# Chunked attention: which products stand between the heads' steps on TensorE, and behind which transposes

## The chip, the core and the metric

The kernel runs on one core of a Trainium2 chip. Five engines work beside each other, each through its own instructions in the order in which they stand: TensorE (PE in the profile) multiplies matrices into PSUM, VectorE (DVE) and ScalarE (ACT) read PSUM and SBUF, GpSimd (POOL) works on SBUF alone, and SyncE (SP) issues the transfers from HBM. An instruction starts when the ones ahead of it on its engine have started and the semaphores that it waits for have been raised. The metric is the device time of one execution in microseconds (us).

## The reference

The program is a network of eight stages on 512 rows of 1024 values. The change lies in the seventh, an attention of 16 heads whose keys and values are shared. In cut form:

```python
def shared_kv(x, kv_norm, w_kv, k_norm):
    h = rmsnorm_2(x, kv_norm)
    kv = (h @ w_kv).reshape(bsz, s, 2, N_HEADS, HEAD_DIM)
    k = rmsnorm_2(kv[:, :, 0], k_norm)
    v = kv[:, :, 1]
...
    def one_chunk(args):
        c, qb = args
        kb = lax.dynamic_slice_in_dim(k_pad, c * CHUNK, BAND, axis=2)
        vb = lax.dynamic_slice_in_dim(v_pad, c * CHUNK, BAND, axis=2)
        sc = jnp.einsum('bhqd,bhkd->bhqk', qb, kb).astype(jnp.float32) * scale + bias
        valid = (c * CHUNK - PAD + jnp.arange(BAND)) >= 0
        sc = jnp.where(valid, sc, -jnp.inf)
        p = jax.nn.softmax(sc, axis=-1).astype(vb.dtype)
        return jnp.einsum('bhqk,bhkd->bhqd', p, vb)
...
            q = (rmsnorm_2(h, b_norm[j]) @ b_w_q[j]).reshape(bsz, s, N_HEADS, HEAD_DIM)
            q = rmsnorm_2(q, b_q_norm[j])
            o = chunk_band_attention(q, k_pad, v_pad, b_rel_bias[j])
            h = h + o @ b_w_o[j]
```

Keys and queries are normed per head, over 64 values: what this norm waits for is at the centre of the prediction.

## The kernel before

Every operand of a product is held as a high and a low part, and `mm3` (lines 148 to 152) makes three matmuls of each product. So a row of line 150, 151 or 152 is a third of a product.

In `attention` (line 883) the 16 heads go in four groups of four; `qt` counts the groups. `quarter` (line 951) makes what a group needs, in steps: `headed(0)` makes the keys, `headed(2)` the queries, `values` the values. Each of the three starts with `project` (line 909), eight steps of twelve matmuls of 256 columns (tiles `ps_mm`, or `ps_s` once) with their weights loaded from HBM, scaled by GpSimd (line 137) and split into high and low parts (lines 140 and 143). After its projection `headed` copies the result out of PSUM (ScalarE, line 917, four copies), squares it (line 920), sums the squares (VectorE, line 921), makes the factors (VectorE line 183, GpSimd line 184), and yields. In its next step it multiplies by the factors (VectorE, line 928, twice) and lets TensorE transpose the two halves into two PSUM tiles (line 933, eight transposes), which are then split into the keys or queries that the heads read. In the same step the next projection begins with its first twelve matmuls.

`heads` (line 326) goes through the 16 steps of a group, four per head with 128, 256, 384 and 512 keys. A step is `scores` (line 269): three matmuls into `ps_s`, the bias and the maximum on VectorE (line 289), the exponentials on ScalarE (line 291), and the division (lines 292 to 296); and, two steps later, `turn` (line 299): transposes of `p` (line 308) into a PSUM tile `ps_t`, its split, and after the fourth step of a head eight matmuls with the values into `ps_o` (line 319). Between them `fill` takes one step of a filler, 36 times per group. The fillers of groups 0 to 2 are `quarter` of the next group; that of group 3 is `values` of group 3 and 48 steps of the output product (`out`, line 964, three matmuls of 512 columns per step).

The tiles `ps_t` have two PSUM buffers that go round in the order of the program; the transposes of line 933 and those of line 308 share them. The tiles `p` have four buffers. What the program's order leaves open is settled by a scheduler when the kernel is built: it takes instructions of higher priority first (the heads' steps have it) and otherwise what it believes to be ready. `issue_after` binds the TensorE instructions made inside it to stand behind a given one. In the kernel before it is used in group 3 alone, from the twentieth step of the filler on. The first and third stages use `heads` too (`mix`, line 361), without it.

Of the kernel before, what the change touches and what calls it, by code (L numbers as in the profile page):

```python
# [65 lines left out]
class Net:  # L66
# [256 lines left out]
            nc.scalar.activation(out=f[a], in_=o[b], func=AF.Copy)  # L323
            it["done"](o[a], f[a], a)

    def heads(self, items, filler, held=99, hi=1000, depth=2):


        pend, marks = [], []

        def turn():
            with self.tc.high_priority(offset=hi):
                self.turn(*pend.pop(0))
            marks.append(self.mark.ins)

        steps = iter(range(99))

        def fill():
            with self.tc.issue_after(marks[-1]) if next(steps) >= held and marks else ExitStack():
                next(filler, None)  # L340

        items[0]["prep"](items[0])
        for n, it in enumerate(items):
            for qb in range(4):
                with self.tc.high_priority(offset=hi):
                    pend.append((it, qb, self.scores(it, qb)))
                fill()
                if len(pend) > depth:
                    turn()
                if qb == 1 and n + 1 < len(items):  # L350
                    items[n + 1]["prep"](items[n + 1])
                fill()
        while pend:
            fill()
            turn()
            fill()
        for _ in filler:
            pass


    def mix(self, l, gnext):
# [10 lines left out]
        with tc.tile_pool(name=f"att{l}", bufs=1, reuse_waits="tile") as ap:  # L372
# [104 lines left out]
            val = [None] * 4  # L477
# [98 lines left out]
            items = [item(hd) for hd in range(8)]  # L576
            prep(items[0])
            items[0]["prep"] = lambda it: None
            gating()
            self.heads(items, branches(), 99, 1000, 2)  # L580
            keep_hp.close()
        with tc.tile_pool(name=f"gate{l}", bufs=1, reuse_waits="tile") as gp:
            self.wide = 0
# [299 lines left out]
    def attention(self, gnext):  # L883
# [3 lines left out]
        with tc.tile_pool(name="att", bufs=1, reuse_waits="tile") as ap:  # L887
# [53 lines left out]
            def values(qt, res):  # L941
                pss = yield from project(1, qt, "mm")
                val = self.t(ap, "v", 2, (P, 4, 2, 4, 64), F32R)
                for i in range(4):
                    if i % 2 == 0:
                        f = self.t(ap, "qr", 3, (P, 2, 4, 64)).rearrange("p n h c -> p n (h c)")
                    S_.activation(out=f[:, i % 2], in_=pss[i // 2][:, i % 2], func=AF.Copy, scale=r[:, i:i + 1])
                    self.split_values(val[:, i], f[:, i % 2])
                res.append(val)

            def quarter(qt, res):
                k, q, v = [], [], []
                yield from headed(0, qt, k)
                yield from headed(2, qt, q)
                res.extend((k, q, v))
                if qt < 3:
                    yield from values(qt, v)

            os_ = [None] * 8
            bias = [self.t(ap, f"bias{n}", 1) for n in range(2)]  # L960
# [3 lines left out]
            def out(k0, nk, c0, n=None):  # L964

                per = 8 // nk
                for i in range(KT):
# [5 lines left out]
                    if n is not None:  # L973
                        self.norm_step(n, i, ALL)

            cur = []
            for _ in quarter(0, cur):
                pass
            for qt in range(4):
                nxt = []  # L980
                k, q, val = cur
                items = []
                for hh in range(4):
                    hd = qt * 4 + hh

                    def prep(it, hd=hd):
                        b = bias[hd % 2]
                        nc.sync.dma_start(out=b[:, 256:], in_=d["bias"][hd])
                        G.tensor_scalar(out=b[:, 256:], in0=b[:, 256:], scalar1=b[:, 256:257], scalar2=None,
                                        op0=ALU.subtract)  # L990
                        G.memset(b[0:64, 448:], NEG)
                        it["bias"] = b

                    def done(o, f, rows, hd=hd):
                        j = hd // 2
                        if hd % 2 == 0:
                            os_[j] = self.pair(ap, "o", 6) if j < 6 else self.pair(ap, "k", 4)
                        V.tensor_tensor(out=f, in0=o, in1=f, op=ALU.add)
                        self.split((os_[j][0][rows], os_[j][1][rows]), f, eng=G)

                    items.append(dict(p=4, step=1 - hh % 2 * 2, q=q[hh // 2], k=k[hh // 2], rows=slice((hh % 2) * 64, (hh % 2) * 64 + 64),
                                      pool=ap, prep=prep, done=done,
                                      v=lambda kb, hh=hh, val=val: val[0][:, kb, hh // 2, hh % 2 * 2:hh % 2 * 2 + 2]))

                def filler():
                    if qt < 3:
                        yield from quarter(qt + 1, nxt)
                    else:
                        yield from values(3, val)
                        yield from out(0, 4, 0)  # L1010
                        yield from out(4, 2, 4)

                self.heads(items, filler(), 20 if qt == 3 else 99, 1000, 2)
                cur = nxt
            n = self.norm_begin(gnext[0])
            for _ in out(6, 2, 6, n):
# [164 lines left out]
```

## Time and profile before

| | |
|---|---|
| time, median of 3 runs | 2823.43 us (2822.30 to 2823.83) |
| the profiled execution | 2822.87 us, of which 2821.1 us are the span of its instructions |
| granted TensorE clock, mean | 0.986 of full speed |
| TensorE busy | 2753.3 us, 98% |
| VectorE, ScalarE, GpSimd busy | 1565.7, 1137.2, 505.3 us |

The attention stands from about 2145 us of the span to 2469 us. A busy TensorE in this profile is not one at its peak: the ends of matmuls are modelled, and a row of 256 columns that shows 0.28 us is followed by the next after 0.12 us. So rows are compared by their starts, and the columns to look at are the starts, the idle time in brackets with what ended it, and the granted clock.

### The profile page before, as it was taken

The numbers are of one execution on the slowest core, as the hardware profiler recorded it, in microseconds if no ns is written. First come the engines' busy times: TensorE is split into PE (matmuls) and PEld (weight loads), VectorE is DVE, ScalarE is ACT, GpSimd is POOL, SyncE is SP. The second block draws the span as 40 slices with busy tenths as digits, with TensorE's granted clock in tenths as the row PEclk, the third lists the DMA queues.
The fourth block names the chain that finished last, engine by engine and source line by source line (L and its number), as shares of the span: only waits on it lengthen the run. The fifth ranks groups of instructions, "written<-read, shape, count | busy, mean of one in ns | idle before, by whom it ended". The sixth has DMA issues, their size and how long they took to land.

```text
span 2821.1 us, 34584 instructions
## 1 busy us (share of the span) xinstructions
PE 2753.3 (98%) x13616; PEld 2315.4 (82%) x13616; DVE 1565.7 (56%) x2371; ACT 1137.2 (40%) x1863; POOL 505.3 (18%) x384
## 2 busy tenths in 40 slices
PE   8999999999999999999999997899999999999999
PEld 7778889888898778888888885788888988788887
DVE  5875556534477764556344579644444777744443
ACT  5553234322255542344222356433323466533222
POOL 5301110100105111101010035300004653200000
PEclk9999999999999999999999999999999999899999
DMA  4113232323322123332323322233332211122322
GB/s 151 63 46 97 95 107 89 93 97 96 96 90 85 50 75 95 101 109 81 98 93 99 111 74 67 67 105 97 97 97 94 79 61 62 51 95 92 100 97 88
DMA packets 77059, 249.70 MB, mean 89 GB/s; under 512 B 8544, under 2 KB 14560, under 8 KB 76896
## 3 DMA queue, kind: packets, MB, share of 16 engines
q1 hardware_dynamic: 76896, 247.49, 27.4%
q8 instruction: 107, 1.75, 0.2%
q14 instruction: 56, 0.46, 0.1%
HBM read 245.36 MB, written 2.10 MB: 88 GB/s over the span
## 4 chain that ended last, share of the span: by engine, by line
PE 86%; DVE 9%; POOL 2%; ACT 1%; DMA 1%; issue 1%; POOLq 0%; DVEq 0%; ACTq 0%
PE ps_mm L151 15%; PE ps_mm L150 15%; PE ps_mm L152 15%; PE ps_s L150 9%; PE ps_s L151 9%; PE ps_s L152 9%; PE ps_o L151 3%; PE ps_o L152 3%; PE ps_o L150 3%; PE ps_o L319 1%; PE ps_t L308 1%; DVE y L745 1%; DMA raw<-in_w_qkv 1%; DVE xl L236 1%; DVE S L213 0%
## 5 line engine op out<-in xcount | busy, mean ns | idle before, releaser
L108 ACT ACTIVATE wh<-raw 128x1024 fp32r<-128x1024 f32 (+3 forms) x391 | 398.8, 1022 | 1175.0 <-PE ps_mm L151 441.0
L109 DVE TENSOR_TENSOR wl<-raw,wh 128x1024 fp32r<-128x1024 f32 (+3 forms) x391 | 498.8, 1278 | 159.2 <-ACT wh L108 155.5
L150 PE MATMUL ps_mm<-xh,wh 128*128 128x512 f32 x1176 | 461.5, 393 | 12.0 <-ACT xh L111 6.8
L151 PE MATMUL ps_mm<-xl,wh 128*128 128x512 f32 x1176 | 460.3, 391 | 0.5 <-DVE xl L112 0.5
L152 PE MATMUL ps_mm<-xh,wl 128*128 128x512 f32 x1176 | 459.9, 391 | 0.0
L150 PEld LDWEIGHTS ps_mm<-xh,wh 128*128 128x128 f32 x1176 | 222.1, 189 | 59.4 <-ACT xh L111 6.8
L151 PEld LDWEIGHTS ps_mm<-xl,wh 128*128 128x128 f32 x1176 | 222.0, 189 | 46.3 <-DVE xl L112 1.0
L152 PEld LDWEIGHTS ps_mm<-xh,wl 128*128 128x128 f32 x1176 | 221.8, 189 | 46.1 <-DVE wl L109 0.3
L152 PE MATMUL ps_s<-xh,wl 128*128 128x512 f32 x552 | 215.4, 390 | 0.0
L150 PE MATMUL ps_s<-xh,wh 128*128 128x512 f32 x552 | 215.2, 390 | 0.0
L151 PE MATMUL ps_s<-xl,wh 128*128 128x512 f32 x552 | 214.8, 389 | 0.0
L150 PE MATMUL ps_mm<-hh,wh 128*128 128x512 f32 (+1 forms) x438 | 167.4, 382 | 0.0
L151 PE MATMUL ps_mm<-hl,wh 128*128 128x512 f32 (+1 forms) x438 | 166.9, 382 | 0.0
L152 PE MATMUL ps_mm<-hh,wl 128*128 128x512 f32 (+1 forms) x438 | 166.9, 382 | 0.0
L680 POOL TENSOR_TENSOR a<-a,rb 128x512 f32<-128x512 f32 x44 | 60.2, 1371 | 534.2 <-DVE a L679 534.2
L614 POOL TENSOR_TENSOR m<-m,g 128x512 f32<-128x512 f32 x48 | 62.7, 1305 | 433.3 <-DVE g L613 433.2
L143 POOL TENSOR_TENSOR wl<-raw,wh 128x1024 fp32r<-128x1024 f32 (+1 forms) x59 | 122.0, 2069 | 62.0 <-ACT wh L140 58.8
L152 PEld LDWEIGHTS ps_s<-xh,wl 128*128 128x128 f32 x552 | 103.6, 188 | 22.3 <-DVE wl L109 1.0
L150 PEld LDWEIGHTS ps_s<-xh,wh 128*128 128x128 f32 x552 | 103.6, 188 | 21.8 <-ACT wh L108 0.5
L151 PEld LDWEIGHTS ps_s<-xl,wh 128*128 128x128 f32 x552 | 103.6, 188 | 21.5
L150 PE MATMUL ps_s<-hh,wh 128*128 128x512 f32 (+1 forms) x300 | 113.9, 380 | 0.0
L151 PE MATMUL ps_s<-hl,wh 128*128 128x512 f32 (+1 forms) x300 | 113.7, 379 | 0.0
(469 smaller groups left out, 5910.4 us busy)
## 6 DMA issues: line engine op xcount, KB each, us to landing
raw<-in_w_in SPq DMA_DIRECT2D x96, 512.0 KB, 3.5
raw<-in_w_gu SPq DMA_DIRECT2D x88, 512.0 KB, 3.5
raw<-in_w_down SPq DMA_DIRECT2D x80, 512.0 KB, 3.6
raw<-in_w_up SPq DMA_DIRECT2D x64, 512.0 KB, 3.4
raw<-in_w_down SPq DMA_DIRECT2D x32, 448.0 KB, 3.3
raw<-in_w_qkv SPq DMA_DIRECT2D x24, 512.0 KB, 3.4
raw<-in_w_out SPq DMA_DIRECT2D x16, 512.0 KB, 3.5
raw<-in_a_w_in SPq DMA_DIRECT2D x16, 512.0 KB, 3.5
```

The source lines that it names most:

```text
L108: a = nc.scalar.activation(out=h, in_=src, func=AF.Copy)
L109: b = (eng or nc.vector).tensor_tensor(out=l, in0=src, in1=h.bitcast(F32), op=ALU.subtract)
L143: eng.tensor_tensor(out=l[:, a:b], in0=raw[:, a:b], in1=h[:, a:b].bitcast(F32), op=ALU.subtract)
L150: mm(out=ps, lhsT=a[0], rhs=b[0], start=first, stop=False)
L151: mm(out=ps, lhsT=a[0], rhs=b[1], start=False, stop=False)
L152: mm(out=ps, lhsT=a[1], rhs=b[0], start=False, stop=last)
L236: lambda: self.nc.vector.scalar_tensor_tensor(out=l, in0=x, scalar=g, in1=h.bitcast(F32), op0=ALU.mult, op1=ALU.subtract))
L308: self.mark = nc.tensor.transpose(out=pt[:, ks], in_=p[:, ks], identity=self.c("ident"))
L319: nc.tensor.matmul(out=o[:, kb * P:], lhsT=it["v"](kb), rhs=pt[:, bs], start=kb == 0 and pt is pth, stop=kb == 3 and pt is ptl)
L614: G.tensor_tensor(out=m, in0=m, in1=g, op=ALU.add)
L680: G.tensor_tensor(out=a, in0=a, in1=rb, op=ALU.mult)
L745: V.scalar_tensor_tensor(out=y, in0=z[:, k:k + T], scalar=cw(k), in1=y, op0=ALU.mult, op1=ALU.add)
```

## The change

`heads` gets a number of steps, `total`, in the place of `held`: at each of its 36 places in a group (68 in `mix`) it takes as many steps of the filler as keep pace with an even spread. In `mix` that is one step per place, as before. In `attention` it is 26 steps for groups 0 to 2 and 48 for group 3. A list `marks` of the last transposes is handed in by `attention` alone and kept over its groups, and with it every step of the filler stands, on TensorE, behind the transposes of line 308 made last. `values` of group 3 now belongs to `quarter` of group 3, so it runs within group 2.

```diff
-    def heads(self, items, filler, held=99, hi=1000, depth=2):
-
-
-        pend, marks = [], []
+    def heads(self, items, filler, total, marks=None, hi=1000, depth=2):
+
+
+        pend = []
+        places, place, given = 8 * len(items) + 2 * depth, 0, 0
 
         def turn():
             with self.tc.high_priority(offset=hi):
                 self.turn(*pend.pop(0))
-            marks.append(self.mark.ins)
-
-        steps = iter(range(99))
+            if marks is not None:
+                marks.append(self.mark.ins)
 
         def fill():
-            with self.tc.issue_after(marks[-1]) if next(steps) >= held and marks else ExitStack():
-                next(filler, None)
+            nonlocal place, given
+            place += 1
+            while given * places < total * place:
+                given += 1
+                with self.tc.issue_after(marks[-1]) if marks else ExitStack():
+                    next(filler, None)
...
-            self.heads(items, branches(), 99, 1000, 2)
+            self.heads(items, branches(), 68)
...
                 res.extend((k, q, v))
-                if qt < 3:
-                    yield from values(qt, v)
+                yield from values(qt, v)
...
+            marks = []
             cur = []
...
                     else:
-                        yield from values(3, val)
                         yield from out(0, 4, 0)
                         yield from out(4, 2, 4)
 
-                self.heads(items, filler(), 20 if qt == 3 else 99, 1000, 2)
+                self.heads(items, filler(), 26 if qt < 3 else 48, marks)
```

Four lines are added ahead of line 937 of the changed kernel, so line 917 reads 921 there, 920 reads 924, and 933 reads 937. Numbers at the end of a tile's name tell tiles of one kind apart. Outside the attention and the first rows of the stage behind it, every engine's instructions stand as they did.

TensorE, kernel before, from the end of the queries' projection of group 1 (`ps_mm_17734` and `ps_mm_17735`) to the first transposes of its result (`qr_17937` and `qr_17943`); the rows left out hold 90 matmuls of the values' projection and steps of the heads:

```order
L152 MATMUL ps_mm_17735<-wh_17847,xl_17044 128x256
L150 MATMUL ps_mm_17983<-wh_17986,xh_16772 128x256
...
L152 MATMUL ps_mm_17983<-wh_18094,xl_17044 128x256
L933 MATMUL ps_t_17965<-tab,qr_17937 128x128 x2
L933 MATMUL ps_t_17965<-tab,qr_17943 128x128 x2
L150 MATMUL ps_mm_17984<-wh_18094,xh_17043 128x256
```

The changed kernel at the same place (`ps_mm_17783` the queries, `ps_mm_18051` and `ps_mm_18052` the values, `qr_18005` and `qr_18011` what is transposed, `p_17951` a head's step):

```order
L152 MATMUL ps_mm_17783<-wh_17891,xl_17044 128x256
L150 MATMUL ps_mm_18051<-wh_18054,xh_16772 128x256
...
L152 MATMUL ps_mm_18052<-wh_18054,xl_16773 128x256
L937 MATMUL ps_t_18033<-tab,qr_18005 128x128 x2
L937 MATMUL ps_t_18042<-tab,qr_18005 128x128 x2
L937 MATMUL ps_t_18033<-tab,qr_18011 128x128 x2
L937 MATMUL ps_t_18042<-tab,qr_18011 128x128 x2
L308 MATMUL ps_t_18073<-tab,p_17951 128x128 x3
L150 MATMUL ps_mm_18051<-wh_18054,xh_16809 128x256
```

Between the last row of the projection and its transposes stand twelve matmuls in place of 90 and the heads' steps among them; the next matmuls of the filler stand behind the head's transposes `ps_t_18073`, and these behind the eight of line 937, whose PSUM buffers they take over. There are six such places, one for the keys and one for the queries of groups 1 to 3. At five of them twelve matmuls stand between; at the first, the keys of group 1, there are two groups of score matmuls and eight matmuls with values besides.

ScalarE, kernel before, around the copies of the same projection (`qr_17943` its second half, `ps_t_17779` and the `p` tiles steps of heads):

```order
L917 ACTIVATE qr_17943<-ps_mm_17735,r_16738 128x256 x2
L140 ACTIVATE wh_18297<-raw_18296 128x1024
L920 ACTIVATE sq_17946<-qr_17943 128x512
L108 ACTIVATE pth_17622<-ps_t_17779 128x4x128
L291 ACTIVATE p_17871,sm_17872<-p_17871,mx_17870 128x512
L291 ACTIVATE p_17911,sm_17912<-p_17911,mx_17910 128x128
```

The same in the changed kernel, up to the split of the transposed queries (line 111):

```order
L921 ACTIVATE qr_18005<-ps_mm_17782,r_16738 128x256 x2
L921 ACTIVATE qr_18011<-ps_mm_17783,r_16738 128x256 x2
L140 ACTIVATE wh_18297<-raw_18296 128x1024
L924 ACTIVATE sq_18008<-qr_18005 128x512
L924 ACTIVATE sq_18014<-qr_18011 128x512
L111 ACTIVATE qh_18038<-ps_t_18033,rv_17068 128x512
L111 ACTIVATE qh_18047<-ps_t_18042,rv_17068 128x512
```

Steps of heads stood between the squares and that split before, and none stands there now.

TensorE, kernel before, heads 12 and 13 (group 3), with no filler among the steps:

```order
L150 MATMUL ps_s_19641<-kh_18505,qh_18754 128x384
L152 MATMUL ps_s_19658<-kh_18505,ql_18755 128x512
L308 MATMUL ps_t_19601<-tab,p_19562 128x128 x3
L308 MATMUL ps_t_19618<-tab,p_19579 128x128 x4
L150 MATMUL ps_s_19704<-kh_19271,qh_19520 128x128
L308 MATMUL ps_t_19654<-tab,p_19595 128x128
L150 MATMUL ps_s_19749<-kh_19271,qh_19520 128x256
```

The changed kernel within group 3 (`oh` and `ol` are finished heads, rows left out are more of the output product):

```order
L150 MATMUL ps_s_20046<-kh_19319,qh_19588 128x512
L308 MATMUL ps_t_19955<-tab,p_19890 128x128 x3
L152 MATMUL ps_mm_19926<-oh_18895,wl_19922 128x512
L308 MATMUL ps_t_19983<-tab,p_19913 128x128 x4
L150 MATMUL ps_mm_19962<-oh_17726,wh_19921 128x512
...
L150 MATMUL ps_s_20073<-kh_19328,qh_19597 128x128
L308 MATMUL ps_t_20039<-tab,p_19946 128x128
L150 MATMUL ps_mm_20030<-oh_18501,wh_20025 128x512
```

The output product, which stood ahead of and behind these heads, now stands among all their steps. Over the stage TensorE changes from one kind of matmul to another 287 times up to the last value matmul, before it was 266.

## Rows read from the trace of the kernel before

**Rows 1.** The page: busy time of the engines, share of the span, instructions.
```profile
PE 2753.3 (98%) x13616; PEld 2315.4 (82%) x13616; DVE 1565.7 (56%) x2371; ACT 1137.2 (40%) x1863; POOL 505.3 (18%) x384
```

**Rows 2.** Windows: length, busy (count) of PE, PEld, DVE, ACT, POOL, PE clock, DMA.
```profile
2340.00:2360.00 20.00, 20.00 (x142) 17.68 (x141) 12.43 (x34) 12.07 (x27) 8.04 (x7) 1.00 0.22 66
...
2380.00:2396.40 16.40, 14.09 (x76) 10.37 (x74) 14.49 (x41) 12.55 (x32) 4.48 (x6) 1.00 0.11 41
2396.40:2420.30 23.90, 23.49 (x75) 17.79 (x76) 13.85 (x50) 15.35 (x40) 6.18 (x9) 0.50 0.06 17
2420.30:2440.00 19.70, 19.14 (x98) 15.08 (x99) 15.32 (x46) 14.28 (x33) 2.87 (x2) 1.00 0.09 27
```

**Rows 3.** Timeline of TensorE in heads 12 to 15: start, length, instruction, idle before.
```profile
2389.66 0.50 PE L319 MATMUL ps_o<-pth,v 128*128 128x512 f32 x1 [0.69 <-ACT pth L108]
...
2395.48 0.32 PE L150 MATMUL ps_s<-kh,qh 64*128 64x128 f32 x1 [0.60 <-DVE mx L289]
```

**Rows 4.** Timeline of TensorE at the queries of group 0.
```profile
2206.32 0.28 PE L150 MATMUL ps_mm<-wh,xh 128*128 128x256 f32 x1
2206.44 0.28 PE L151 MATMUL ps_mm<-wl,xh 128*128 128x256 f32 x1
2206.64 0.63 PE L933 MATMUL ps_t<-tab,qr 128*128 128x128 f32 x4
2207.03 0.36 PE L152 MATMUL ps_mm<-wh,xl 128*128 128x256 f32 x1
2208.86 0.66 PE L933 MATMUL ps_t<-tab,qr 128*128 128x128 f32 x4 [1.47 <-DVE qr L928]
2209.27 0.36 PE L150 MATMUL ps_mm<-wh,xh 128*128 128x256 f32 x1
```

**Rows 5.** Timeline of ScalarE at the queries of group 1.
```profile
2241.63 0.84 ACT L917 ACTIVATE qr<-ps_mm,r 128x256 f32<-128x256 f32 x2
2242.34 1.07 ACT L140 ACTIVATE wh<-raw 128x1024 fp32r<-128x1024 f32 x1
2243.29 0.65 ACT L920 ACTIVATE sq<-qr 128x512 f32<-128x512 f32 x1
```

**Rows 6.** Timeline of VectorE there.
```profile
2244.15 0.67 DVE L921 TENSOR_REDUCE sc<-sq 128x8 f32<-128x512 f32 x1
...
2245.36 0.17 DVE L183 TENSOR_SCALAR rs_v<-sc 128x16 f32<-128x16 f32 x1
...
2249.05 2.99 DVE L928 TENSOR_TENSOR qr<-qr,fac 128x512 f32<-128x512 f32 x2
```

**Rows 7.** Timeline of GpSimd there.
```profile
2245.60 2.90 POOL L184 TENSOR_TENSOR fac<-rs_v,half 128x16 f32<-128x16 f32 x1 [0.22 <-DVE rs_v L183]
```

**Rows 8.** Timelines of ScalarE: copies at the queries of group 3, keys of group 2.
```profile
2372.12 0.84 ACT L917 ACTIVATE qr<-ps_mm,r 128x256 f32<-128x256 f32 x2 [2.55 <-PE ps_t L933]
...
2277.54 0.85 ACT L917 ACTIVATE qr<-ps_mm,r 128x256 f32<-128x256 f32 x2
```

**Rows 9.** Timelines of VectorE at the same two.
```profile
2379.73 1.49 DVE L928 TENSOR_TENSOR qr<-qr,fac 128x512 f32<-128x512 f32 x2 [0.35 <-POOL fac L184]
...
2288.73 3.12 DVE L928 TENSOR_TENSOR qr<-qr,fac 128x512 f32<-128x512 f32 x2
```

**Rows 10.** Timeline of TensorE: the two longest waits after the start, in another stage.
```profile
1730.05 0.77 PE L150 MATMUL ps_mm<-xh,wh 128*128 128x512 f32 x1 [5.03 <-DVE y L778]
...
1779.74 0.80 PE L150 MATMUL ps_s<-U,wh 128*128 128x512 f32 x1 [4.34 <-ACT U L111]
```

**Rows 11.** Windows around these two waits, columns as in rows 2.
```profile
1727.40:1730.00 2.60, 0.00 (x0) 0.00 (x0) 2.60 (x3) 0.00 (x0) 2.60 (x2) 0.50 0.21 19
1730.00:1737.60 7.60, 5.19 (x11) 3.64 (x12) 7.60 (x7) 1.86 (x4) 5.12 (x3) 0.50 0.34 115
...
1775.00:1779.70 4.70, 0.40 (x2) 0.00 (x0) 4.54 (x6) 1.86 (x3) 2.93 (x2) 0.88 0.00 0
1779.70:1785.40 5.70, 5.66 (x13) 4.09 (x14) 4.83 (x6) 2.91 (x5) 1.00 (x1) 0.50 0.01 3
```

## The prediction, made before the run

> **What bounds the kernel now.** I read the page first: TensorE is busy 98% of the span, the next engine 56% [rows 1]. So a change of order can win only where TensorE waits or runs at its lower clock, and it loses wherever it makes TensorE wait. I then cut the attention into windows. At 2340 to 2360 us TensorE has no idle time and the full clock, 142 matmuls in 20.00 us; at 2396.4 to 2420.3 it has 75 in 23.90 us at a granted clock of 0.50, which is 1.2 GHz [rows 2]. The timeline says what stands there: heads 12 to 15 alone. The 20 steps of the filler that may slide ahead have been used up before, and TensorE waits for the softmax chain again and again, 0.69 us for a split on ScalarE, 0.60 us for a maximum on VectorE [rows 3], until the clock falls. What the change can win is this stretch. What it can lose is read elsewhere: at the places where TensorE transposes keys and queries that the norm must first have finished. At the queries of group 0 it waits there 1.47 us for the multiplication of line 928, and the next matmul, which needs nothing of it, starts only behind these transposes, at 2209.27 [rows 4]. 98 matmuls of other work stood between that projection and the transposes, and even so it waited.
>
> **What goes.** Over 2380 to 2440 us TensorE is idle for 16.40 - 14.09 = 2.3, 23.90 - 23.49 = 0.4 and 19.70 - 19.14 = 0.6 us, together 3.3 us. In the middle window it works 23.49 us at half clock, which full clock would do in half, so 11.7 us are lost to the clock. Together 15.0 us [rows 2]. In the changed order the 48 steps of the output product stand among the sixteen steps of these heads; three matmuls of 512 columns each cover the chain of a step. I take 14 us as won, 10 if some waits stay, 15 at most.
>
> The number of matmuls is the same. Their kinds alternate 21 times more (287 against 266); one alternation costs about 0.1 us more than going on (the start of the transposes comes 0.20 us behind a matmul that goes on to its like after 0.12, and the way back costs about as much [rows 4]). That is +2 us, between 0 and 4. In `mix` one step still falls on each place and no marks are handed in, so nothing moves there: 0. The values of group 3 are the same eight steps in either kernel, and stood ahead of heads 12 to 15 already: 0, covered by the group-2 heads' steps; uncovered they would be 96 matmuls of 0.12, 11.5 us, which TensorE has to spend in any case. Their weights' loads on SP's queue and scaling on GpSimd move with them; GpSimd is busy 8.04 of 20 us there [rows 2], so that too is 0.
>
> **What comes: six waits of TensorE.** Before, when a projection was done, TensorE went on with the next one while ScalarE, VectorE and GpSimd normed the result. Ninety matmuls, with steps of heads among them, stood ahead of the queries' transposes in group 1. Now the filler's matmuls stand behind the last transposes of the heads. Those go round the same two PSUM buffers as the transposes of keys and queries, so they can't go ahead of these. So when the norm's chain is not done, TensorE has only the twelve matmuls of the same step to do, and then everything is queued behind the eight transposes: the head's transposes, the rest of the next projection, and soon the heads' `p` buffers, which only these transposes free.
>
> How long is the chain? At the queries of group 1: the second pair of copies starts at 2241.63, then a weight copy of 1.07 us stands in front of the second square [rows 5]; the sum ends at 2244.15 + 0.67, line 183 starts at 2245.36, line 928 ends at 2249.05 + 2.99 = 2252.04 [rows 6], and 2.90 us of it are the power on GpSimd [rows 7]. That is 10.4 us from the copies to the end of the multiplications. The shortest of eight such chains is 2379.73 + 1.49 - 2372.12 = 9.1 us, the longest 2288.73 + 3.12 - 2277.54 = 14.3 us [rows 8, 9]. In the changed order none of the heads' instructions stands between, but the weight copy does; I take 9.7 us, between the shortest chain and the one of rows 5 to 7. With nothing queued anywhere the pieces alone make 0.84 (copies) + 1.3 (two squares) + 0.67 + 0.17 + 2.90 + 1.49 = 7.4 us [rows 5 to 7, 9], which I keep as the lower bound; 14.3 is the upper.
>
> From the start of the last matmul of the projection to the copies go at least the 0.28 us that its row lasts, and 0.06 us pass from the multiplications' end at 2208.80 to the transposes at 2208.86 [rows 4]. Against that stand 13 matmuls of 0.12 us, 1.56 us (the last one and the twelve), and four transposes of 0.39 us [rows 4] that may run while the second multiplication does. The wait is 0.28 + 9.7 + 0.06 - 1.56 - 0.39 = 8.1 us, between 5.8 and 12.7. At five places this holds. At the first, the keys of group 1, six score matmuls and eight value matmuls stand in front besides; at 0.12 us [rows 4] to 0.20 us (19.70 us for 98 matmuls [rows 2]) they cover 1.7 to 2.8 us, say 2.3. So the first wait is 5.8 us (3.5 to 10.4), and the sum is 5 x 8.1 + 5.8 = 46.3 us, between 32 and 74.
>
> **The clock behind each wait.** After a wait of 5.03 us TensorE's clock was at half for 7.6 us more, in which it was busy for 5.19, and after one of 4.34 us for 5.7 us, busy for 5.66 [rows 10, 11]. Half of that busy time is lost, 2.6 and 2.8 us. The wait of 1.47 us above had no such end. Waits of 6 to 8 us are longer than both that did, so I take 2.8 us for each of six: +17 us, with 0 (the clock holds) and 23 us (half of 7.6 each) as ends. The Trainium skill says the same of kernels whose matmuls come in bursts ("TensorE: Matmul & The Clock Gate", section "HAM oscillation — how this bites in real kernels"): the price of coming back from the low clock is paid at every break, once per burst. By that rule six breaks cost six times, as taken here; if the clock were to hold, as it did at 1.47 us, the sum would be 17 us lower. Two falls behind two long waits speak for the rule here.
>
> **The sum.** Against the profiled execution, 2822.9 us: - 14 + 2 + 46.3 + 17 = + 51, so 2874 us. The median of the runs is 0.6 us above the profiled one, which makes 2875.
>
> **The rivals.**
> 1. *Short chains.* While TensorE stands still the other engines empty their queues, the chains come down to their bare 7.4 us and the clock hardly falls: - 14 + 2 + 32 and 0 to 6 for the clock, 2843 to 2849. For it: nothing of heads stands between on ScalarE. Against it: no chain of the trace is under 9.1 us, with engines that were hardly loaded [rows 8, 9].
> 2. *Long chains.* GpSimd's scaling of the next weights falls together with line 928, which took 2.99 us for its two instructions in one place and 1.49 in another [rows 6, 9], and less of the old loss is won: - 10 + 2 + 74 + 23, 2912. Against it: the long chains stood in a stretch where heads' steps came between.
> 3. *The transposes don't wait, and the kernel is faster.* Then only the bare stretch goes: 2822.9 - 15 + 2 = 2810. This decides as soon as the chain from the last matmul to the transposes is shorter than what covers it, 13 matmuls and four transposes, 2.0 us. For it: TensorE is busy at 98%, and with an even spread each step of a head has cover. Against it: the shortest chain is 9.1 us, and at 98 matmuls of cover TensorE still waited [rows 4].
> 4. *Gain and loss cancel.* The 12 us net gain would be used up by six waits of 2 us with no fall of the clock, 2823. Against it the same rows; it needs chains of 4 us, less than GpSimd's power and the two multiplications take alone (2.90 + 1.49 [rows 7, 9]).
>
> **How the numbers follow.** The forecast (2855 to 2897: chains of 8 to 12 us, the clock falling each time) gets 0.68, short chains 0.14, long ones 0.13, the faster case 0.03, cancelling 0.02. The predicted time is the forecast's, 2875. The range is 2847 to 2903: the forecast, most of the short chains and a part of the long ones. About 0.2% (5.6 us) is what a measurement of this kernel can tell from no change. Faster 0.03, same 0.02, slower 0.95.
>
> **What would show it.** In the changed kernel's trace: six rows of the eight transposes (line 937 there) with idle time in front, ended by VectorE's line 932, about 8 us each and less at the first; windows of half clock that begin in these waits and end some 6 us behind them; no half clock and little idle time between the last projection and the end of the output product, where heads 12 to 15 stand; `mix` as it was. If the waits are there but shorter than 6 us, the chain was mis-sized; if they are there and the clock holds, the clock's term was wrong; if TensorE runs matmuls of the next projection ahead of the transposes, the reading of the order was wrong, and with it the sign. If heads 12 to 15 still run at half clock, the 14 us were wrong.

## The result, and the profile after

The changed kernel takes 2886.29 us (median of 4 runs, 2882.35 to 2890.18), the kernel before 2823.63 us in runs beside it (4 runs, 2822.30 to 2824.05). The ratio is 1.0221 with a 95% interval of 1.0209 to 1.0234: slower by 62.7 us. The profiled execution took 2882.35 us, its span 2880.1, against 2822.9 and 2821.1 before.

The page first; the columns are those of [rows 1], and the second row is TensorE's granted clock in 40 slices of the span:

```profile
PE 2763.9 (96%) x13616; PEld 2319.5 (81%) x13616; DVE 1554.4 (54%) x2371; ACT 1138.9 (40%) x1863; POOL 503.0 (17%) x384
...
PEclk9999999999999999999999998999999888999999
```

TensorE is busy 10.6 us longer than in [rows 1] with the same 13616 instructions, and the span is 59.0 us longer. So some 48 us are new idle time and the rest is work that takes longer, in good part at a lower clock; the three 8s side by side are the slices from 2232 to 2448 us.

The waits of TensorE between 2210 and 2520 us, from the second group of heads to the end of the output product:

```profile
engine line waited for: us in total, times, longest us
PE ps_t L937 <- DVE qr L932: 44.6, 9, 8.1
PE ps_t L308 <- DVE ql L112: 3.4, 3, 1.1
PE ps_t L308 <- DVE kl L109: 3.0, 3, 1.0
PE ps_mm L150 <- ACT kh L108: 2.1, 1, 2.1
```

Each row says which instruction waited, for which result, how long in all, how often, and the longest wait. Line 937 is the eight transposes, line 932 the multiplication. The nine waits belong to six places: 8.1, 7.6, 7.8, 7.6, 6.6 and 6.9 us; at three places the wait is in two pieces, since the first four transposes need only the first multiplication. The next two rows are new: the heads' transposes (line 308) queue behind the eight, and wait again, about 1 us each time, until the split of what the eight wrote has freed the PSUM buffer. One such place, the queries of group 1, in TensorE's timeline (as [rows 4], which show the queries of group 0):

```profile
2267.92 1.11 PE L937 MATMUL ps_t<-tab,qr 128*128 128x128 f32 x4 [6.31 <-DVE qr L932]
2270.32 1.09 PE L937 MATMUL ps_t<-tab,qr 128*128 128x128 f32 x4 [1.28 <-DVE qr L932]
2272.54 0.90 PE L308 MATMUL ps_t<-tab,p 128*128 128x128 f32 x3 [1.14 <-DVE ql L112]
2273.09 0.56 PE L150 MATMUL ps_mm<-wh,xh 128*128 128x256 f32 x1
```

No matmul of the next projection stands between the three waits; the first is at 2273.09. What TensorE waited for there is told by the chain that ended last, followed back through this place (start, length, engine and what):

```profile
2259.34 0.13 PE ps_mm L152
...
2259.49 1.57 ACT qr L921 x4
2261.06 0.95 ACT wh L140
...
2262.04 0.69 DVE wl L143
2262.73 1.20 DVE sc L925 x2
...
2263.96 0.19 DVE rs_v L183
...
2264.21 2.94 POOL fac L184
...
2267.17 3.00 DVE qr L932 x2
...
2270.32 0.67 PE ps_t L937 x2
```

Before the change these steps lay beside TensorE's work [rows 5 to 7]; now they are the path: copies, the split of the next weights (lines 140 and 143), sums, power, multiplication, 10.7 us from 2259.49 to 2270.17. GpSimd's power and the two multiplications are more than half of it.

Windows of half clock, and the last heads (columns as in [rows 2]):

```profile
2232.50:2242.70 10.20, 4.66 (x21) 4.27 (x22) 6.50 (x9) 1.86 (x5) 3.94 (x3) 0.50 0.04 13
2266.60:2276.90 10.30, 6.56 (x29) 5.79 (x30) 6.08 (x10) 2.48 (x6) 2.61 (x2) 0.50 0.02 6
2317.80:2328.10 10.30, 6.15 (x27) 5.38 (x28) 5.75 (x12) 2.24 (x6) 3.22 (x2) 0.50 0.05 21
2348.60:2362.20 13.60, 7.18 (x32) 6.41 (x33) 6.87 (x13) 3.07 (x6) 5.02 (x2) 0.50 0.11 39
2399.80:2413.40 13.60, 7.76 (x32) 6.73 (x32) 5.98 (x17) 2.85 (x8) 3.72 (x2) 0.50 0.13 39
2433.90:2444.10 10.20, 5.51 (x25) 5.11 (x26) 4.37 (x9) 2.47 (x5) 2.77 (x1) 0.50 0.11 44
2444.10:2520.00 75.90, 73.38 (x385) 57.83 (x384) 48.69 (x120) 41.31 (x89) 12.35 (x12) 1.00 0.19 61
```

Six windows, one at each wait, and TensorE worked 37.8 us in them, half of which full clock would have saved: 18.9 us. The last row is heads 12 to 15 with the output product among their steps: the clock stays full, and TensorE is idle 2.5 us of 75.9. The 23.9 us of half clock of [rows 2] are gone.

### The profile page after: what moved, and what is told of

Its sections match the earlier page's. It is cut to its first block, busy times and chain, and to the rows that moved or that the text cites. A ratio compares the mean times of both kernels' runs of the same rounds, so it can differ in the third digit from the quotient of the medians.

```text
span 2880.1 us, 34567 instructions
## 1 busy us (share of the span) xinstructions
PE 2763.9 (96%) x13616; PEld 2319.5 (81%) x13616; DVE 1554.4 (54%) x2371; ACT 1138.9 (40%) x1863; POOL 503.0 (17%) x384
## 4 chain that ended last, share of the span: by engine, by line
PE 86%; DVE 8%; POOL 2%; ACT 2%; issue 1%; DMA 1%; POOLq 0%; DVEq 0%; ACTq 0%
PE ps_mm L151 15%; PE ps_mm L150 15%; PE ps_mm L152 15%; PE ps_s L150 9%; PE ps_s L151 9%; PE ps_s L152 9%; PE ps_o L151 3%; PE ps_o L152 3%; PE ps_o L150 3%; PE ps_o L319 1%; PE ps_t L308 1%; DVE y L749 1%; DMA raw<-in_w_qkv 1%; POOL fac L184 1%; DVE qr L932 1%
## 5 line engine op out<-in xcount | busy, mean ns | idle before, releaser
L618 POOL TENSOR_TENSOR m<-m,g 128x512 f32<-128x512 f32 x48 | 62.7, 1306 | 432.6 <-DVE g L617 432.5
```

Of the source, the lines that this page charges most:

```text
L618: G.tensor_tensor(out=m, in0=m, in1=g, op=ALU.add)
```

## Where the time went

I cut one stretch out of every trace but those of e5 and e10, which order group 0 otherwise: from the first transposes of line 933 (937 after) in group 0 to the last matmul of the output product. Its length is idle time, the time lost to half clock (half of what TensorE worked there), and the rest. These are sums over the timelines and the clock of each trace, in us. "Rest" is thus the work, counted at full clock. The second column is the number of TensorE's instructions, in the order in which they stand in the kernel, between the last matmul of a projection of keys or queries and its transposes, least and most at the six places of groups 1 to 3.

| kernel | between | length | idle before the eight transposes | other idle | half clock, lost to it | rest |
|---|---|---|---|---|---|---|
| before | 100 to 248 | 277.3 | 1.5 | 4.0 | 23.9, 11.7 | 260.0 |
| after | 12 to 26 | 338.7 | 46.0 | 8.9 | 68.3, 18.9 | 264.8 |
| e1_no_lock | 100 to 222 | 272.7 | 1.5 | 5.7 | 6.8, 2.6 | 262.9 |
| e2_lock_last | 100 to 204 | 279.9 | 2.7 | 5.2 | 20.5, 9.9 | 262.1 |
| e3_values_back | 12 to 107 | 332.8 | 38.7 | 11.0 | 71.7, 20.7 | 262.4 |
| e4_late | 69 to 86 | 300.0 | 17.0 | 6.7 | 37.5, 16.1 | 260.2 |
| e6_filled_waits | 52 to 66 | 334.8 | 16.7 | 9.9 | 34.1, 14.7 | 293.5 |
| e7_lock_third | 55 to 72 | 320.9 | 25.3 | 10.4 | 51.2, 19.7 | 265.4 |
| e8_late_seventh | 108 to 128 | 277.1 | 3.0 | 9.5 | 3.4, 1.7 | 262.8 |
| e9_late_no_lock | 127 to 218 | 276.1 | 1.5 | 6.1 | 13.7, 5.7 | 262.8 |

After against before is 61.4 us longer in this stretch, and the span 59.0; the 2.4 us between lie outside it. The 61.4 us are 44.5 of waits before the eight transposes, 4.9 of other waits, 7.2 of clock (18.9 - 11.7) and 4.8 of rest.

## The experiments

My theory: the rule that holds the filler's products behind the heads' last transposes ("the lock" below, `issue_after` with `marks`) makes the waits, since it leaves some twelve matmuls between a projection and its transposes while the norm's chain takes some 10 us. Rivals: the even spread itself makes them; the eight values made one group ahead make them; the clock would have fallen in any case. Unless something else is said, edits are made on the changed kernel and everything is computed.

**The spread without the lock.**

```
-                self.heads(items, filler(), 26 if qt < 3 else 48, marks)
+                self.heads(items, filler(), 26 if qt < 3 else 48)
```

> The changed kernel with the even spread and the early values, but without the lock: the filler's matmuls may stand ahead of the last transposes again. Theory (the lock makes TensorE wait for the norm): the six waits before the eight transposes, 44.6 us in the changed kernel, fall to under 4 us in all, none of the six half-clock windows is left, and the time is 2808 to 2826 us. Rival (the even spread itself, fewer steps ahead of the transposes, makes the waits): at least 20 us of waits stay and the time is over 2850 us.

Measured: 2821.27 us (10 runs, 2818.74 to 2824.39), ratio to before 0.9993 [0.9983, 1.0002]. Its waits of TensorE from 2185 us to the end of the output product, the longest of them:

```profile
PE ps_mm L150 <- ACT kh L108: 2.1, 1, 2.1
PE ps_t L937 <- DVE qr L932: 1.5, 1, 1.5
```

The one row left of the eight transposes is the 1.5 us of group 0, which the kernel before has too [rows 4]. So the six waits need the lock; the spread and the earlier values don't make them without it. (The lock with the old filling, one step at each place, was not run.) Nor would the clock have fallen in any case: of the six windows none is left, and the one that there is, 6.8 us, lies at the end of the output product. The second reading is as useful: the spread alone gains next to nothing. The stretch of the table loses 9.1 us less to the clock, but there are 1.7 us more idle and 2.9 us more rest: 4.6 us gained in the trace, 2 by the ratio of the runs, whose interval holds 1.

**The lock in the last group alone.**

```
-                self.heads(items, filler(), 26 if qt < 3 else 48, marks)
+                self.heads(items, filler(), 26 if qt < 3 else 48, marks if qt == 3 else None)
```

> The changed kernel with the lock in the last group alone (heads 12 to 15, with the output product), none in groups 0 to 2. Theory: the waits at the keys and queries are gone as without any lock, and the output product stands among the steps of heads 13 to 15, so the half-clock stretch of the kernel before (23.9 us) is gone or short: 2808 to 2820 us. Rival (the lock costs time in the last group as well, since products wait for the softmax chain): slower than without any lock by 5 us or more.

Measured: 2825.49 us (10 runs, 2823.11 to 2830.49), ratio 1.0013 [1.0003, 1.0022]: above my range, and 4.2 us above e1, just short of the rival's 5. The six waits are gone, but the half clock is still there, at 2391 us:

```profile
PE ps_t L308 <- DVE ql L112: 2.0, 1, 2.0
...
2380.00:2390.90 10.90, 8.75 (x47) 6.36 (x46) 8.41 (x26) 7.63 (x21) 2.49 (x3) 1.00 0.12 44
2390.90:2408.00 17.10, 16.57 (x50) 11.78 (x49) 9.86 (x33) 10.17 (x25) 3.52 (x5) 0.50 0.06 17
```

In the 10.9 us before it TensorE was idle for 2.2 us, 2.0 of them in one wait of the heads' transposes behind the split of the queries of group 3. In the groups without the lock the filler of group 2 slides ahead and is used up; from 2382.2 to 2404.6 us the trace shows no matmul of a filler among the steps of heads. The output product, locked, doesn't come forward to stand in for it; without the lock in this group (e1) the clock stays full from 2380 to 2440 us. A lock that begins late left a hole ahead of itself here.

**The values of group 3 back in group 3.**

```
-                yield from values(qt, v)
+                if qt < 3:
+                    yield from values(qt, v)
...
+                        yield from values(3, val)
                         yield from out(0, 4, 0)
...
-                self.heads(items, filler(), 26 if qt < 3 else 48, marks)
+                self.heads(items, filler(), (26, 26, 18, 56)[qt], marks)
```

> The changed kernel with the values of group 3 put back into group 3 (18 steps in group 2, 56 in group 3); lock and even spread stay. Theory (moving the values costs and saves nothing by itself): 2886 us within 6, the same six waits of 42 to 48 us. Rival (a part of the loss comes from the fuller group 2): 10 us or more faster.

Measured: 2880.43 us (4 runs, 2878.19 to 2884.27), ratio 1.0207 [1.0192, 1.0222], 6 us under the changed kernel by the medians and 4 by the ratios, whose intervals overlap. I had expected the same six waits. The row of the waits, with group 0's 2.9 us:

```profile
PE ps_t L937 <- DVE qr L932: 38.7, 10, 8.1
```

Four are as they were (8.1, 7.6, 7.8 and 7.6 us); at the keys of group 3, 21 instructions of TensorE stand between the projection and its transposes, where 12 stood, and the wait is 4.7 us in place of 6.6; at the queries of group 3, 107 stand there, and the wait of 6.9 us is gone. The stretch is 5.9 us shorter. So where the values stand is worth a few us of 63, by cover at these two places.

**The chain made longer: the power of the factors made twice on GpSimd.** The same line is added to both kernels, the changed one and the one before; the second power overwrites the first with the same factors.

```
                 self.rsqrt(fac, st.rearrange("p n h -> p (n h)"), 16, 1.0 / 64)
+                self.rsqrt(fac, st.rearrange("p n h -> p (n h)"), 16, 1.0 / 64)
```

> The changed kernel with the factors of keys and queries made twice (lines 183 and 184 repeated, the same result), so 0.2 + 2.9 us more on VectorE and GpSimd in each of the eight chains of the norm. Theory (this chain ends the six waits): each wait grows by the 3.1 us, 6 x 3.1 = 19 us, and about 3 us come in group 0, where TensorE waits for the same line already: 2904 to 2914 us, with the same six half-clock windows. Rival (the waits end by something else, the GpSimd work is hidden): under 2892 us.

> The kernel before the change, with the power of the factors on GpSimd made twice, as e5_power_twice has it in the changed one. Everything is computed. Theory (before the change the products that are not held cover the chain, so that a longer one costs only where a wait stands already, the 1.47 us of group 0): 1 to 6 us over the kernel before, 2823 to 2830. Rival (the chain's length counts at all six places, as it did in the changed kernel, whose six waits grew by 22 us): 2840 to 2850.

Measured, on the changed kernel: 2912.17 us (4 runs, 2910.88 to 2913.50), ratio 1.0314 [1.0299, 1.0330], 25.9 us over the changed kernel. On the kernel before: 2825.26 us (11 runs, 2819.98 to 2827.18), ratio 1.0003 [0.9994, 1.0012]. The row of the eight transposes in the waits of TensorE, of the changed kernel with two powers (the line is one further down):

```profile
PE ps_t L938 <- DVE qr L933: 68.3, 9, 11.5
```

and of the kernel before with two powers (the first row is a wait for the PSUM buffer, until a head's split has freed it):

```profile
PE ps_t L934 <- DVE ptl L109: 1.1, 1, 1.1
PE ps_t L934 <- DVE qr L929: 0.8, 2, 0.5
```

Of the 68.3 us 3.6 are group 0's, whose order is not the same as with one power, in either kernel; it is left out of what follows. The six waits grew from 44.6 to 64.7 us, 3.3 us each, where lines 183 and 184 take 3.1 [rows 6 and 7]: about a us of TensorE for every us of the chain, once the lock is there. From the last matmul of the keys' projection of group 1 to the end of the output product the trace is 19.7 us longer, 20.1 us of waits and 1.8 more lost to the clock, against 1.8 less rest and 0.4 less other idle time. The profiled execution is 31.2 us longer than that of the changed kernel, which was the fastest of its four; the 11.5 us outside this stretch lie mostly in and ahead of group 0, 2.2 of them waits and 4.6 a window of half clock that the changed kernel doesn't have there. Without the lock on these groups the same extra power, eight times over, cost nothing that can be measured. There the transposes also moved back when the kernel was built: 142 to 279 instructions stand in front of them at the six places, where 100 to 248 stood with one power. In the locked kernel 12 to 26 stand there with either.

**The lock two steps looser: behind the transposes of two steps earlier.**

```
-                with self.tc.issue_after(marks[-1]) if marks else ExitStack():
+                with self.tc.issue_after(marks[-3]) if marks and len(marks) >= 3 else ExitStack():
```

> The changed kernel with the filler locked behind the last transposes but two, in place of the last. So 36 matmuls and some steps of heads stand between a projection and its transposes, in place of twelve. Theory (wait is the chain less its cover): the cover grows from 2 us to 6 to 8 us, the waits fall from 44.6 us to 10 to 25 us in all, and the time is 2830 to 2860 us. Rival (any lock costs the same, as it makes TensorE follow the heads): 2880 us or more.

Measured: 2866.32 us (4 runs, 2863.78 to 2868.32), ratio 1.0149 [1.0132, 1.0166]: 20 us under the changed kernel, but 6 us above my range. The row of the waits:

```profile
PE ps_t L937 <- DVE qr L932: 25.3, 12, 5.9
```

With 55 to 72 instructions between a projection and its transposes, in place of 12 to 26, the waits fall by 20.7 us. The clock's loss doesn't fall with them (19.7 after 18.9): shorter waits, but a window of half clock at each of the six places, as before, and one more at the end of the output product. That is what my range missed.

**The transposes written later, with the lock.** The multiplication and the eight transposes, which stood right behind `headed`'s one step, are put into a function that the next projection calls before its fifth (e4) or seventh (e8) step.

```
+            self.late = None
+            LATE_AT = 4                      # e8: 6
...
                     for k in range(4):
+                        if LATE_AT == 4 * c + k and self.late:
+                            finish()
...
                 yield
+                self.late = (raws, fac, which, res)
+
+            def finish():
+                raws, fac, which, res = self.late
                 for i in range(2):
```

> The changed kernel, all of it, but the multiplication by the factors and the eight transposes are written four steps later, after the fifth step of the next projection, so 60 matmuls and more stand between a projection and its transposes. Theory: the waits before the transposes are gone (under 3 us in all), no half-clock window stays in the attention, and what the even spread wins in heads 12 to 15 is seen alone: 2805 to 2816 us. Rival (the lock costs by holding products back from any wait of the softmax chain): the waits at the eight transposes go, but 10 us or more of waits before the heads' transposes of line 308 come, and the time is over 2825 us.

> As the run with the transposes four steps later, but after the seventh step of the next projection instead of the fifth, so 84 matmuls and several steps of heads stand before them (with 60 the chains grew to 11.5 to 13.9 us, since steps of heads stood between, and 17.0 us of waits and 34 us at half clock stayed). Theory: the waits at the eight transposes fall under 6 us, of which 2.5 are those of group 0, no half-clock window comes in groups 1 to 3, and what the even spread wins in heads 12 to 15 is left alone: 2808 to 2820 us. Rival (with the lock the time stays above the kernel before whatever the transposes do): 2830 us or more.

Measured: before the fifth step 2849.29 us (4 runs, 2847.21 to 2853.25), ratio 1.0097 [1.0082, 1.0112], a clear miss; before the seventh 2822.97 us (10 runs, 2819.76 to 2827.07), ratio 1.0003 [0.9994, 1.0013], above my range as well. At the fifth step the six waits are 14.7 us in all, none at the first place and 1.3 to 4.0 us at the others, and the clock still falls behind four of these five. The rows are the waits, with group 0's 2.3 us, and one window:

```profile
PE ps_t L946 <- DVE qr L941: 17.0, 9, 3.8
...
2315.60:2322.40 6.80, 4.67 (x21) 4.27 (x22) 4.30 (x7) 2.49 (x5) 2.44 (x2) 0.50 0.23 80
```

The rival's time came true and its mechanism didn't: the heads' transposes wait 3.3 us, not 10. With steps of heads between, their instructions on ScalarE and VectorE stand between the chain's own, and it grows from 8.2 to 12.6 us to 11.1 to 13.9; 69 to 86 instructions don't cover that at five places of six. I had counted the cover and not that the cover lengthens the chain. At the seventh step, with 108 to 128, the waits are gone, and 3.4 us of half clock are left, yet the kernel is no faster than before. Its waits of TensorE from 2180 us on:

```profile
PE ps_t L308 <- DVE kl L109: 3.7, 3, 1.3
PE ps_t L946 <- DVE qr L941: 3.0, 2, 1.6
PE ps_mm L150 <- ACT kh L108: 2.1, 1, 2.1
PE ps_s L150 <- ACT qh L111: 1.9, 3, 1.5
```

3.0 us are group 0's. The others are not in the kernel before: heads' transposes behind the split of the keys, scores behind the split of the queries, and the output product behind the split of the last heads, after which nothing is left to stand in front. The 10.0 us of clock that are saved against before go into 7.1 us of idle time and 2.8 us of rest.

**Late and without the lock.** The edits of e8 and e1 together.

> The multiplication and the eight transposes of a projection of keys or queries are written after the seventh step of the next projection, as in e8_late_seventh, and the heads' steps give no marks, as in e1_no_lock: no product is held behind the heads' transposes. Everything is computed. Theory (the lock alone makes the waits; without it the copies' chain is covered whether the transposes are written early or late): no wait of the eight transposes over 2.5 us, time within 4 us of e1_no_lock's 2821, 2817 to 2825. Rival (the late transposes take something by themselves, since the waits of the heads' transposes behind keys and queries that e8_late_seventh has, 3.7 us, come from where the transposes are written and not from the lock): 2826 to 2832.

Measured: 2822.45 us (11 runs, 2820.18 to 2832.65), ratio 1.0006 [0.9997, 1.0015]; waits of the eight transposes 1.5 us, all in group 0, as the theory said:

```profile
PE ps_t L946 <- DVE qr L941: 1.5, 1, 1.5
```

It is not faster than e1, and no version here beats the kernel before by more than can be measured.

**The waits filled with other matmuls.** Forty matmuls of 256 columns are added at each of the six places, into the buffer that the transposes then overwrite, so that TensorE works where it stood still:

```
                     ps = self.ps("t")
+                    for _ in range(40 if qt and j == 0 else 0):
+                        nc.tensor.matmul(out=ps[:, :256], lhsT=xs[0][0][:, :P], rhs=xs[1][0][:, :256], start=True,
+                                         stop=True)
```

> The changed kernel with 40 more matmuls of 256 columns, whose result is overwritten, ahead of the eight transposes in groups 1 to 3: 40 x 0.12 = 4.8 us of TensorE work inside each of the six waits. Theory (each wait costs twice, once as idle time and once through the clock behind it): the waits left are 1.5 to 3 us, the half-clock windows are gone in at least four of the six places, and the time falls by 12 to 19 us although TensorE does 29 us more work: 2866 to 2875 us. Rival (the idle time alone costs): 2886 us within 5.

Measured: 2882.68 us (4 runs, 2880.46 to 2887.36), ratio 1.0212 [1.0197, 1.0227]: 3.6 us under the changed kernel, where I had expected 11 to 20. The time lies in the rival's range. The waits shrank as intended, from 46.0 to 16.7 us, and the 240 matmuls took their place in the rest (28.7 us more). The clock did not hold: 4.2 us less were lost to it, not the 12 to 19 that the theory needs. The row of the waits, and two windows, each with the 10 us before it:

```profile
PE ps_t L940 <- DVE qr L932: 16.7, 10, 2.1
...
2309.40:2319.40 10.00, 8.03 (x68) 7.83 (x66) 3.53 (x7) 4.31 (x9) 8.28 (x5) 1.00 0.17 54
2319.40:2329.60 10.20, 7.91 (x32) 6.53 (x32) 5.87 (x13) 2.84 (x8) 1.66 (x1) 0.50 0.00 0
2394.80:2404.80 10.00, 8.00 (x66) 7.59 (x65) 3.35 (x6) 4.18 (x8) 6.02 (x3) 1.00 0.16 54
2404.80:2411.60 6.80, 5.81 (x27) 5.19 (x26) 3.56 (x12) 2.84 (x8) 0.00 (x0) 0.50 0.00 0
```

Behind a wait of 2.0 us in each of these the clock was at half for 10.2 and 6.8 us. Filling most of a wait didn't keep the clock up. Whether filling all of it would was not tried.

## Why the prediction was right, and which terms were off

The prediction was 2875 us with 2847 to 2903, slower; 2886.3 is 11 us above it and inside the range. The terms, predicted and measured in the profiled execution, by the table:

| term | predicted | measured |
|---|---|---|
| waits before the eight transposes | +46.3 (32 to 74) | +44.6 |
| clock behind them | +17 (0 to 23) | +18.9 |
| bare stretch of heads 12 to 15 | -14 (-15 to -10) | -13.2 |
| alternations of kinds (the rest) | +2 (0 to 4) | +4.8 |
| the heads' transposes behind the eight | none | +6.4 |
| sum | +51 | +61.5 |

**The waits** were right in place, releaser and sum. Two errors in them partly cancelled. At five places I had 8.1 us and they were 36.5 / 5 = 7.3: the last two chains were short, 8.2 and 8.8 us from the third copy to the end of the multiplications, and the three between 9.9 against the 9.7 assumed. Most of that difference is the multiplication itself. VectorE and GpSimd at the queries of group 1, and VectorE at those of group 3:

```profile
2267.17 2.99 DVE L932 TENSOR_TENSOR qr<-qr,fac 128x512 f32<-128x512 f32 x2 [3.04 <-POOL fac L184]
2267.55 2.07 POOL L137 TENSOR_TENSOR raw<-raw,prm 128x1024 f32<-128x1024 f32 x1 [0.41 <-DMA raw<-in_w_qkv]
...
2436.71 1.29 DVE L932 TENSOR_TENSOR qr<-qr,fac 128x512 f32<-128x512 f32 x2 [3.11 <-POOL fac L184]
```

At the three places of 9.9 us the pair takes 2.99 us and GpSimd's scaling of the next weights (line 137) runs beside it, as rival 2 had it; at the last two it takes 1.29 us and nothing runs on GpSimd. No run changed this alone, so that the one slows the other is not shown. At the first place I had 5.8 us, for the cover of six score and eight value matmuls, and it was 8.1: there heads' instructions stood among the chain's, which took 12.6 us. What the cover gives it can also take, as e4 showed again. e1 shows that the waits don't come without the lock; e5 and e10 show that the chain's length counts about one for one in the locked kernel and not measurably in the kernel before.

**The clock** fell at each of the six, for 10.2 to 13.6 us, at 3.2 us lost each time (18.9 / 6) where I took 2.8 from [rows 11]. The windows begin inside the waits, so part of each lies over idle time and costs nothing. The Trainium skill's rule ("TensorE: Matmul & The Clock Gate", section "HAM oscillation — how this bites in real kernels"), that a kernel whose matmuls come in bursts pays for the low clock at every burst, agrees with the six windows for six waits. By my reading of [rows 4 and 10] a short wait would have paid nothing. This holds for the 1.4 us of group 0 here, and it fails in e4 and e6, where half clock began behind waits of 1.8 to 3.8 us.

**The bare stretch** was right for the locked kernel: 11.7 us of clock and the 4.0 us of other idle time (0.8 of them ahead of these heads, at 2320 to 2340 us) are gone, and 2.5 us of idle time in 2444 to 2520 us stand against them, 2.1 of which are the wait at the end of the output product: the products that stood behind the last heads are used up by then. As a gain of the spread by itself it was too much. Without the lock (e1) the whole stretch gains 4.6 us, with the lock and covered transposes (e8) 0.2 us.

**The term that was missing** comes from the list of what is queued behind the eight transposes. I named the heads' transposes and the buffers that they share with the eight, and then ended the wait where the eight end. But the buffer comes free only when ScalarE and VectorE have split what the eight wrote (0.70 and 0.76 us in the chain above), so each of the six places has a second wait of 1.0 to 1.1 us, 6.4 us in all, and 9 of the 10 us that the sum is short are this and the next term. e1 and the kernel before have no row of these waits.

**The alternations** were costed by their number, 0.1 us each. The rest grew by 4.8 us in the changed kernel, by 2.1 in e2 and by 2.9 in e1, while the kinds alternate 20, 28 and 11 times more than in the kernel before (counted in the traces). So the number of alternations is not what the rest goes by; what its 2 to 5 us are is open.

**The median**: the profiled execution of the changed kernel was the fastest of its four, 3.9 us under their median, where I had added 0.6. That is a part of the 11 us which no term of the mechanism could give.

Of the rivals, the first and the second fall by the sum of the waits (32 and 74 there), the third and the fourth by the waits themselves. The third one's case, no waits and no bare stretch, is seen in e8, and it gives 2823 there and not the 2810 that I had worked out. `mix` and everything else ahead of the attention is as it was: the stretch begins 3 us earlier than in the kernel before, and what follows it is 0.7 us longer.

## What to carry to other kernels

Where a scheduler holds one queue of work behind another's steps, look for the instruction in the held queue that waits for a slow chain on other engines, and count what the in-order engine can still do once it stands at the head: here twelve matmuls against 10 us, where 69 to 86 instructions left waits at five places of six (e4) and 108 to 128 left none (e8). What can slide is cover that doesn't show in the profile: in the kernel before seven of eight chains were hidden, and with a longer chain more was put in front (e10). And follow a wait to where its buffer comes free, not to where the waiting instruction ends.

## What the runs showed of the hardware that I had not expected

TensorE's clock fell to half also where the waits were short: in e6 behind waits of 2.0 us, for 6.8 and 10.2 us, and in e4 behind waits of 2.1 to 3.8 us, for 6.8 to 10.2 us, though the wait of 1.5 us in [rows 4] and the 1.4 us in the same place after the change left it at full. Nor does the length of the one wait decide it: the same wait of 2.1 us stands at the end of the output product in most of these kernels. In e4 3.4 us of half clock followed it; in the changed kernel and in e8 the clock stayed full (windows from the end of that wait on, in this order):

```profile
2482.90:2486.30 3.40, 3.39 (x8) 2.49 (x9) 0.69 (x1) 0.05 (x1) 1.27 (x1) 0.50 0.01 4
...
2516.80:2530.00 13.20, 12.80 (x54) 10.09 (x55) 10.60 (x13) 8.09 (x13) 7.30 (x5) 1.00 0.14 43
...
2454.00:2466.00 12.00, 11.52 (x49) 9.01 (x50) 9.59 (x12) 6.78 (x13) 7.55 (x5) 1.00 0.11 30
```

What decides it there is open. Waits cut from 46.0 to 25.3 us (e7) left the loss to the clock where it was (18.9 and 19.7 us), so it doesn't shrink in step with the waits. Without them it went to 2.6 and 1.7 us in e1 and e8, but e2 and e9, which lack them too, still lost 9.9 and 5.7 us in and behind the last heads.
